# Reading 512-column operands in four passes of 16-byte granules, and moving those operands in SBUF

## The chip, the cores and the metric

The kernel runs on one core of one Trainium2 chip. The metric is device time in microseconds (us) of one execution, from the first to the last instruction with what lies around it. The time before is the median of three executions, 838.82 us (838.07 to 838.83). About 0.2% (1.7 us) is what a measurement of this kernel can tell from no change.

## The reference

One encoder layer on an input x of 512 positions by 1024 channels, all in float32:

```
x = x + 0.5 * swiglu(rms_norm(x, g1), w_gate1, w_up1, w_down1)      # 1024 -> 2752 -> 1024
u = rms_norm(x, g2) @ w_in                                          # fourier 512 | q 8x64 | k 2x64 | v 2x64
a = fourier_mixer(u[:512])                                          # Re(DFT2) per group, then a 128x128 map
b = gqa_attention(u[512:])                                          # head norms, rotary, softmax over 512 keys
x = x + concat([a, b]) @ w_out
x = x + 0.5 * swiglu(rms_norm(x, g3), w_gate2, w_up2, w_down2)
y = rms_norm(x, g4)
```

where swiglu(h, g, u, d) is (silu(h @ g) * (h @ u)) @ d.

## The kernel before

Everything is held transposed: a tile has 128 channels as its partitions and the 512 positions along them. A float32 factor is split into a high part in the matmul's own rounded format and a low part that holds the rest, and a product of two factors is three matmuls: high by high, high by low, low by high. `product` (L172) issues the three (L173, L175, L176). The stationary operand is a 128x128 block of weights, the moving one 512 positions (2048 bytes of each partition) or 256, and the result is a PSUM bank.

The layer runs in three stages.

1. The first feed-forward part (`ffn`). A first group of hidden blocks goes by plain products: `gate` multiplies the 8 pairs `hh[k]`, `hl[k]` (high and low parts of the scaled input) by weights; `opening1` does the same for the first four blocks in an order of its own (L693). All further hidden blocks go by `seven`: a seven-product scheme on half-size blocks, whose matmuls are in `multiply` (L407), with moving operands of 256 columns from the tile `rt` and weights in 4096-byte slots of the tile `ring`. Each group ends with the down products (`down`, L173 to L176, and L487 and L488 for the last 64 hidden channels), whose moving operands are the 512-column activations in the tile `at`.
2. The mixer. Six projections (`k`, `q0` to `q3`, `v`) multiply `hh` and `hl` by weights through `product`; the Fourier projections (L998 to L1000) use `hh` and `hl` as stationary operands against 256-column weights; then attention (L1134, L1135, L1160, L1203), the position transform (L1057) and the output projection.
3. The second feed-forward part, whose last group ends by halves: the last three output blocks do the first 256 positions by `product` and the rest by `by_tokens` (L519).

The order on TensorE is the order of the program text in the feed-forward parts and a list written out by hand in the mixer; it does not depend on where tiles lie.

The tile `ring` holds twelve slots for weights. `hh[k]` and `hl[k]` lie in slot k of the same tile (eight of the twelve), so weights and moving operands share it. `room(pool, n)` puts an unused tile of n bytes between others to set where the next one starts. `FURTHER` moves the Fourier weights and `SKIP` the weights of the last three down blocks, in elements of 4 bytes. In `multiply`, one matmul in each run of `seven` is cut in two, of 64 and 192 columns (`CUT`).

As built, the ring's slots start at byte 16512 of the partition, `at` at 119168 and `rt` at 148032. Taken modulo 64 all three are 0; modulo 128 `rt` lies 64 away from the slots.

Of the kernel before, what the change touches and what calls it, by code (L numbers as in the profile page):

```python
# [7 lines left out]
F32R = mybir.dt.float32r  # L8
# [5 lines left out]
P = 128  # L14
S = 512
D = 1024
KD = D // P
# [4 lines left out]
HD = 64  # L22
EPS = 1e-6
WARM = 9
FURTHER = 48
FURTHER_IN = "f0", "f1", "f2", "f3"
ROOM = 64
NS = 12

GROUPS1 = ((0, "t", 1, 2), range(3, 9), range(9, 15), range(15, 21))  # L30
# [3 lines left out]
USES = "a11", "a12", "s1", "s2", "s4", "s3", "a22"  # L34
PIECES = (0, 2, 2, 0, 2, 1, 1)
KH = KD // 2
SKIP = 16
LAST = 3
CUT = 1, P // 2
HI_DVE = ("f0", "f1")  # L40
# [43 lines left out]
def encoder(ctx, tc, A, out):  # L84
    nc = tc.nc
    cp = ctx.enter_context(tc.tile_pool(name="const", bufs=1))
    wp = ctx.enter_context(tc.tile_pool(name="weights", bufs=3))

    ring = cp.tile([P, NS * KD * P + 2 * ROOM], F32R, name="ring")
    taken = []  # L90

    def room(pool, n):


        pool.tile([P, n // 4], F32, name=f"room{len(rooms)}")
        rooms.append(n)
# [11 lines left out]
    gains = gx[:, : 4 * KD].rearrange("p (n k) -> p n k", k=KD)  # L108
    xt = gx[:, 4 * KD :].rearrange("p (k s) -> p k s", s=S)
    x = [xt[:, k, :] for k in range(KD)]  # L110
    hh = [ring[:, k * KD * P : k * KD * P + S] for k in range(KD)]
    hl = [ring[:, k * KD * P + S : (k + 1) * KD * P] for k in range(KD)]


    def in_order():
# [9 lines left out]
    def slot_at(tile, i, rooms=0):  # L125
        o = i * KD * P + rooms * ROOM
        return tile[:, o : o + KD * P]

    slots = [slot_at(ring, i, int(i >= KD + 2)) for i in range(NS)]

    def further(tile, i, rooms=0):
        o = i * KD * P + rooms * ROOM + FURTHER
        return tuple(tile[:, o + j * KD * P : o + (j + 1) * KD * P].rearrange("p (a b) -> p a b", b=P) for j in range(2))
# [21 lines left out]
    def parts_of(n):  # L155

        return (slice(0, CUT[1]), slice(CUT[1], HALF)) if n == CUT[0] else (slice(0, HALF),)

    def weights(src, name, n=KD, raw=None, by_dma=False, skip=0):
        raw = raw or raw_tile(src, name, n)  # L160
        hi, lo = weight_slots(n, skip)
        if name in HI_DVE:
            nc.vector.tensor_copy(hi[:, :n, :], raw[:, :n, :])
        else:
            nc.scalar.copy(hi[:, :n, :], raw[:, :n, :])  # L165
        if by_dma:
            rest_by_dma(lo, hi, src)
        else:
            lows(lo[:, :n, :], raw[:, :n, :], hi[:, :n, :])
        return hi, lo  # L170

    def product(ps, whi, wlo, mhi, mlo, first, last, cut=False):  # L172
        nc.tensor.matmul(ps, whi, mhi, start=first, stop=False)  # L173
        for t in parts_of(CUT[0]) if cut else (slice(0, ps.shape[-1]),):
            nc.tensor.matmul(ps[:, t], whi, mlo[:, t], start=False, stop=False)  # L175
        nc.tensor.matmul(ps, wlo, mhi, start=False, stop=last)  # L176
# [92 lines left out]
    def ffn(norm, after, wgu, wd, wdt, groups, opening, closing):  # L269
# [4 lines left out]
        n_ = norm.n  # L274
        n_plain = len(groups[0])
        with tc.tile_pool(name=f"act{n_}", bufs=1) as ap, tc.tile_pool(name=f"sums{n_}", bufs=2) as sp:
            room(ap, 192)
            at = ap.tile([P, PLACES, 2, S], F32R, name=f"at{n_}")
            room(ap, 192)
            rt = ap.tile([P, 7, 2, KH, HALF], F32R, name=f"rt{n_}")  # L280
            wt, raws = [], {}
            free, where = list(range(PLACES)), {}
# [12 lines left out]
            def gate(c, between={}, by_dma=False):  # L295
                whi, wlo = weights(wgu[c], f"gu{n_}_{c}", by_dma=by_dma)
                ps = bank(f"gu{n_}_{c}")
                for k in range(KD):
                    between.get(k, int)()
                    product(ps, whi[:, k, :], wlo[:, k, :], hh[k], hl[k], k == 0, k == KD - 1)  # L300
                return ps

            def tail_weights():
# [168 lines left out]
            def down(d, group, gi):  # L472

                js = [j for j in group if j != "t"]
                src, halves_ = wd[d][:, js[0] : js[-1] + 1, :], closing and gi == len(groups) - 1 and d >= KD - LAST
                raw = raws[d] = raw_tile(src, f"dn{n_}_{d}_{gi}", len(js))
                whi, wlo = weights(src, "", len(js), raw, skip=SKIP if halves_ else 0)
                if halves_:
                    token_weights(d, js)
                w = wt[d // 4][:, d % 4 * P : (d % 4 + 1) * P]  # L480

                def steps(ps, t):
                    for i, j in enumerate(group):
                        h, l = (at[:, where[j], o, t] for o in range(2))
                        first, last = i == 0, i == len(group) - 1
                        if j == "t":
                            nc.tensor.matmul(ps[:, t], w, h, start=first, stop=False)  # L487
                            nc.tensor.matmul(ps[:, t], w, l, start=False, stop=last)  # L488
                        else:
                            k = j - js[0]  # L490
                            cut = first and d == KD - LAST and t == slice(0, HALF)
                            product(ps[:, t], whi[:, k, :], wlo[:, k, :], h, l, first, last, cut)
                        yield

                return steps
# [36 lines left out]
            every = slice(0, S)  # L532
            for gi, group in enumerate(groups):
                last = gi == len(groups) - 1
# [3 lines left out]
                else:  # L538
# [3 lines left out]
                    pss = dict(enumerate(opening(gate, lambda: norm.column([norm.acc]), lambda: row.append(norm.row()))))  # L542
# [4 lines left out]
                    for i, c in enumerate(left):  # L547
# [6 lines left out]
                        while len(parts) * len(left) > (len(left) - 1 - i) * KH:  # L554
                            o = parts.pop(0)
# [14 lines left out]
                for d in range(KD):  # L570
# [8 lines left out]
                    ps = bank(f"dn{n_}_{d}_{gi}")  # L579
# [66 lines left out]
    cut = [0] + [4 * KD + k * S for k in (1, 2, 4, 6, 8)]  # L646
# [23 lines left out]
    def opening1(gate, column, row):  # L670

        pss = [bank(f"gu0_{c}") for c in range(4)]
        ws = []

        def highs(i, k):
            n0.scale_high(k, None if k else nc.vector)
            hi, _ = ws[i]
            for c in (slice(0, 2), slice(2, 4)) if k == 0 else (slice(0, 4),):
                nc.scalar.copy(hi[:, k % 2, c], raws[i][:, k % 2, c])

        def weight_lows(i, k):
            hi, lo = ws[i]
            lows(lo[:, k % 2], raws[i][:, k % 2], hi[:, k % 2])

        def products(k):
            hi, lo = ws[k // 2]
            passes = [(c, w, m) for w, m in ((hi, hh), (hi, hl), (lo, hh)) for c in range(4)]
            for n, (c, w, m) in enumerate(passes):
                if (k, n) == (6, 8):
                    sums()  # L690
                if (k, n) == (7, 4):
                    row()
                nc.tensor.matmul(  # L693
                    pss[c], w[:, k % 2, c], m[k], start=k == 0 and m is hh and w is hi,
                    stop=k == KD - 1 and w is lo,
                )

        ss = []

        def sums():  # L700
            ss.append(bank("ss0"))
            for c in range(4):
                n0.sum(ss[0], c, [n0.acc])

        with tc.manual_schedule(engines={mybir.EngineType.Activation, mybir.EngineType.DVE}):
            for k in range(KD):
                i = k // 2
                if k % 2 == 0:
                    ws.append(tuple(slot().rearrange("p (a c b) -> p a c b", a=2, b=P) for _ in range(2)))
                highs(i, k)  # L710
                if k < KD - 1:
                    n0.scale_low(k)
                    weight_lows(i, k)
                for j in {3: range(0, 4), 5: (4, 5), 6: (6, 7)}.get(k, ()):
                    n0.sums(j)
            for k in range(KD - 1):
                products(k)
            n0.scale_low(KD - 1)
            n0.mean(ss[0], 0, 4)
            n0.power(0, 4)  # L720
            weight_lows(KH - 1, KD - 1)
            products(KD - 1)
        nc.sync.dma_start(out=qkg, in_=A["qkg"])
        nc.sync.dma_start(out=fb, in_=A["fb"])
        return [pss[0:2], pss[2:4]]
# [6 lines left out]
    with tc.tile_pool(name="mix", bufs=1) as mp, tc.tile_pool(name="mixt", bufs=1) as mt:  # L732

        room(mp, 192)
        more_tile = mp.tile([P, 2 * KD * P + ROOM], F32R, name="more")
        more = [slot_at(more_tile, i) for i in range(2)]
# [63 lines left out]
        banks, rots, swaps, owns, sqs = {}, {}, {}, {}, {}  # L800

        def project_ops(c, name):

            weight_ops(f"w{name}", A["wins"][c])

            def step(k):
                if k == 0:
                    banks[name] = bank_for(name, {"v": 1, "k": 3, "q0": 3}.get(name, 2))
                whi, wlo = ws[f"w{name}"]
                product(banks[name], whi[:, k, :], wlo[:, k, :], hh[k], hl[k], k == 0, k == KD - 1)  # L810

            for k in range(KD):
                op(f"{name}.{k}")(lambda k=k: step(k))
# [514 lines left out]
    first, rest = out[0].rearrange("p (k s) -> p k s", s=HALF), out[1].rearrange("p (c n) -> p c n", n=D)  # L1328
# [222 lines left out]
```

## Time and profile before

| | |
|---|---|
| median of 3 executions | 838.82 us |
| span of the profiled execution | 836.5 us |
| outside the span (median less span) | 2.3 us |
| TensorE matmuls | 829.6 us busy, 99% of the span |
| VectorE | 640.0 us, 77% |
| ScalarE | 465.3 us, 56% |
| TensorE clock granted | 0.999 |

The only time of the profiled execution itself is its span; the last instructions end with it, so the 2.3 us beside it is launch and end. A matmul's own duration in the profile contains its latency: a 512-column matmul shows 389 ns, while the next one starts some 227 ns later. What a stream of matmuls costs is read from the starts in the timeline (the distance from one start to the next, here called the pace), not from the mean durations. A line of the timeline gives the start in us from the span's start, the stretch in us, the engine, the line, the operation, the tiles and the count.

### The profile page before, as it was taken

What the parts mean: (1) busy time and instruction counts of PE and PEld (TensorE: products, weight loads), DVE (VectorE), ACT (ScalarE), POOL (GpSimd) and SP (SyncE); (2) the same over time, 40 slices, a digit from 0 to 9 for tenths busy, and PEclk for the clock granted to TensorE, in tenths of its full rate; (3) what the DMA queues carried; (4) which work ended last, traced back from release to release, by engine and by line L of the source; (5) the groups of instructions that cost most, each with busy time, mean ns of one, the idle gap of its engine ahead of it and who ended that gap; (6) DMA issues with size and microseconds to landing.
All of it is one profiled execution on the core that took longest, in us unless ns stands there. A gap on an engine that the chain in (4) does not pass through costs nothing.

```text
span 836.5 us, 13664 instructions
## 1 busy us (share of the span) xinstructions
PE 829.6 (99%) x5406; PEld 751.5 (90%) x5406; DVE 640.0 (77%) x1005; ACT 465.3 (56%) x778; POOL 30.7 (4%) x34
## 2 busy tenths in 40 slices
PE   9999999999999999999999999999999999999997
PEld 6888998899989998888998888899988999899986
DVE  7898896489746947699998488999954896479573
ACT  7763664167524645677786356656622673257462
POOL 0110000000000000221100000100000000000001
PEclk9999999999999999999999999999999999999999
DMA  7664322323242213532020224443232332322222
GB/s 254 171 149 161 129 89 76 120 101 139 76 138 95 67 54 114 169 99 80 26 76 26 74 86 130 114 164 121 89 120 89 133 112 66 131 102 95 68 75 101
DMA packets 31168, 89.58 MB, mean 107 GB/s; under 512 B 3712, under 2 KB 8832, under 8 KB 31104
## 3 DMA queue, kind: packets, MB, share of 16 engines
q1 hardware_dynamic: 27776, 82.61, 29.0%
q0 software_dynamic: 2608, 5.12, 3.3%
q10 hardware_dynamic: 720, 0.98, 0.3%
q8 instruction: 42, 0.69, 0.3%
q14 instruction: 22, 0.18, 0.1%
HBM read 84.24 MB, written 2.10 MB: 103 GB/s over the span
## 4 chain that ended last, share of the span: by engine, by line
PE 98%; issue 0%; DMA 0%; DVE 0%; ACT 0%; POOLq 0%; POOL 0%; DVEq 0%
PE r L407 23%; PE q L407 11%; PE dn L175 9%; PE dn L173 9%; PE dn L176 9%; PE p L407 6%; PE mix L173 3%; PE mix L175 3%; PE mix L176 3%; PE gu L693 3%; PE gu L173 3%; PE gu L176 3%; PE gu L175 3%; PE mix L1203 2%; PE mix L1160 2%; PE mix L1134 1%
## 5 line engine op out<-in xcount | busy, mean ns | idle before, releaser
L407 PE MATMUL r<-rt,ring 128*128 128x256 f32 x1686 | 209.6, 276 | 0.0
L407 PEld LDWEIGHTS r<-rt,ring 128*128 128x128 f32 x1686 | 200.6, 188 | 0.9
L175 PE MATMUL dn<-at,ring 128*128 128x512 f32 x300 | 116.7, 389 | 0.0
L176 PE MATMUL dn<-at,ring 128*128 128x512 f32 x300 | 116.7, 389 | 0.0
L173 PE MATMUL dn<-at,ring 128*128 128x512 f32 x300 | 116.7, 389 | 0.0
L407 PE MATMUL q<-rt,ring 128*128 128x256 f32 x840 | 106.6, 276 | 0.0
L123 DVE TENSOR_TENSOR ring<-s,ring 128x1024 fp32r<-128x1024 f32 x70 | 85.5, 1221 | 24.1 <-ACT ring L366 20.8
L407 PEld LDWEIGHTS q<-rt,ring 128*128 128x128 f32 x840 | 100.4, 188 | 0.0
L528 DVE SCALAR_TENSOR_TENSOR gx<-dn,gx 128x512 f32<-128x512 f32 x61 | 41.9, 689 | 74.3 <-PE dn L176 74.3
L366 ACT CAST ring<-s 128x1024 fp32r<-128x1024 f32 x70 | 73.5, 1050 | 28.0 <-PE p L407 13.7
L165 ACT CAST ring<-raw_dn 128x768 fp32r<-128x768 f32 (+3 forms) x58 | 45.4, 786 | 76.7 <-PE dn L175 60.4
L176 PEld LDWEIGHTS dn<-at,ring 128*128 128x128 f32 x300 | 56.3, 188 | 11.8
L173 PEld LDWEIGHTS dn<-at,ring 128*128 128x128 f32 x300 | 56.3, 188 | 11.3
L175 PEld LDWEIGHTS dn<-at,ring 128*128 128x128 f32 x300 | 56.3, 188 | 11.2
L123 DVE TENSOR_TENSOR ring<-raw_dn,ring 128x768 fp32r<-128x768 f32 (+3 forms) x58 | 51.6, 892 | 5.9 <-PE r L407 4.6
L407 PE MATMUL p<-rt,ring 128*128 128x256 f32 x420 | 53.3, 276 | 0.0
L123 DVE TENSOR_TENSOR ring<-raw_g,ring 128x1024 fp32r<-128x1024 f32 x35 | 42.7, 1219 | 10.4 <-PE p L407 10.3
L407 PEld LDWEIGHTS p<-rt,ring 128*128 128x128 f32 x420 | 50.2, 188 | 0.0
L366 ACT CAST ring<-raw_g 128x1024 fp32r<-128x1024 f32 x35 | 36.8, 1053 | 13.9 <-DMA raw_g<-in_wgu 8.3
L415 ACT COPY p<-r 128x256 f32<-128x256 f32 x35 | 12.9, 370 | 49.1 <-PE r L407 48.7
L439 ACT ACTIVATE g<-g 128x512 f32<-128x512 f32 x35 | 22.2, 633 | 23.4 <-DVE g L438 23.1
L375 ACT CAST ring<-raw_u 128x512 fp32r<-128x512 f32 x35 | 21.8, 624 | 16.8 <-PE q L407 15.9
(318 smaller groups left out, 1557.1 us busy)
## 6 DMA issues: line engine op xcount, KB each, us to landing
raw_g<-in_wgu SPq DMA_DIRECT2D x35, 512.0 KB, 3.6
raw_u<-in_wgu SPq DMA_DIRECT2D x35, 512.0 KB, 4.3
raw_dn<-in_wd SPq DMA_DIRECT2D x40, 384.0 KB, 3.1
raw_gu<-in_wgu SPq DMA_DIRECT2D x12, 512.0 KB, 3.5
raw_o<-in_wo SPq DMA_DIRECT2D x8, 512.0 KB, 3.5
raw_dn<-in_wd SPq DMA_DIRECT2D x8, 448.0 KB, 3.3
raw_wq<-in_wins SPq DMA_DIRECT2D x4, 512.0 KB, 4.4
raw_f<-in_winf SPq DMA_DIRECT2D x4, 512.0 KB, 4.0
```

Of the source, the lines that this page charges most:

```text
L123: nc.vector.tensor_tensor(out=lo, in0=src, in1=asf(hi), op=ALU.subtract)
L165: nc.scalar.copy(hi[:, :n, :], raw[:, :n, :])
L173: nc.tensor.matmul(ps, whi, mhi, start=first, stop=False)
L175: nc.tensor.matmul(ps[:, t], whi, mlo[:, t], start=False, stop=False)
L176: nc.tensor.matmul(ps, wlo, mhi, start=False, stop=last)
L366: nc.scalar.copy(hi, src)
L375: nc.scalar.copy(hi, src)
L407: nc.tensor.matmul(ps[:, t], a[:, ks], b[:, i, t], start=first and i == 0 and o == 0, stop=i == KH - 1 and o == 2, skip_group_check=not first,
L439: nc.scalar.activation(b["g"], b["g"], AF.Silu)
L528: nc.vector.scalar_tensor_tensor(out=x[d][:, t], in0=ps[:, t], scalar=0.5, in1=x[d][:, t], op0=ALU.mult, op1=ALU.add)
L693: nc.tensor.matmul(pss[c], w[:, k % 2, c], m[k], start=k == 0 and m is hh and w is hi, stop=k == KD - 1 and w is lo,)
L1160: nc.tensor.transpose(pts[n][:, c * P : (c + 1) * P], prob[t, b, c][:, kc * P : (kc + 1) * P], ident)
```

## The change

The products that read a 512-column moving operand from `at`, `hh` or `hl` through `gate`, `opening1`, `down` (not its last halves) and the mixer's six projections read it, and write PSUM, in another order: instead of columns 0 to 511, four passes, each of which takes 4 columns (16 bytes) out of every 16 (64 bytes): columns 0 to 3, 16 to 19, and so on, then 4 to 7, 20 to 23, and so on. The number of columns, matmuls and weight loads stays. `hh` and `hl` start 48 bytes below the slots, and the rooms, `FURTHER` and `SKIP` are set with the same distance in mind.

```diff
-FURTHER = 48
+FURTHER = 36
+FRONT, NEAR = 16, 4
-SKIP = 16
+SKIP = 4
...
-    ring = cp.tile([P, NS * KD * P + 2 * ROOM], F32R, name="ring")
+    whole = cp.tile([P, FRONT + NS * KD * P + 2 * ROOM], F32R, name="ring")
+    ring = whole[:, FRONT:]
...
-    hh = [ring[:, k * KD * P : k * KD * P + S] for k in range(KD)]
-    hl = [ring[:, k * KD * P + S : (k + 1) * KD * P] for k in range(KD)]
+    hh, hl = (
+        [whole[:, k * KD * P + o * S + NEAR : k * KD * P + (o + 1) * S + NEAR] for k in range(KD)] for o in range(2)
+    )
...
+    def turned(ap):
+        return ap.rearrange("p (a b c) -> p b a c", b=4, c=4)
+
-    def product(ps, whi, wlo, mhi, mlo, first, last, cut=False):
+    def product(ps, whi, wlo, mhi, mlo, first, last, cut=False, turn=False):
+        if turn:
+            ps, mhi, mlo = turned(ps), turned(mhi), turned(mlo)
+            for a, b in ((whi, mhi), (whi, mlo), (wlo, mhi)):
+                nc.tensor.matmul(ps, a, b, start=first and b is mhi and a is whi, stop=last and a is wlo)
+            return
...
-            room(ap, 192)
+            room(ap, 144)
             at = ap.tile([P, PLACES, 2, S], F32R, name=f"at{n_}")
-            room(ap, 192)
+            room(ap, 240)
             rt = ap.tile([P, 7, 2, KH, HALF], F32R, name=f"rt{n_}")
...
-                    product(ps, whi[:, k, :], wlo[:, k, :], hh[k], hl[k], k == 0, k == KD - 1)
+                    product(ps, whi[:, k, :], wlo[:, k, :], hh[k], hl[k], k == 0, k == KD - 1, turn=True)
...
+                        turn = t == every
...
-                            product(ps[:, t], whi[:, k, :], wlo[:, k, :], h, l, first, last, cut)
+                            product(ps[:, t], whi[:, k, :], wlo[:, k, :], h, l, first, last, cut, turn)
...
                 nc.tensor.matmul(
-                    pss[c], w[:, k % 2, c], m[k], start=k == 0 and m is hh and w is hi,
+                    turned(pss[c]), w[:, k % 2, c], turned(m[k]), start=k == 0 and m is hh and w is hi,
...
-                product(banks[name], whi[:, k, :], wlo[:, k, :], hh[k], hl[k], k == 0, k == KD - 1)
+                product(banks[name], whi[:, k, :], wlo[:, k, :], hh[k], hl[k], k == 0, k == KD - 1, turn=True)
```

As built, the pools round every tile's size up to a multiple of 32 bytes, so the rooms of 144 and 240 bytes take 160 and 256. The places that follow, with the distance from the ring's slots modulo 64 and modulo 128:

| | slots start | `hh`, `hl` from the slots | `at` from the slots | `rt` from the slots |
|---|---|---|---|---|
| before | 16512 | 0 / 0 | 0 / 0 | 0 / 64 |
| after | 16576 | 16 / 80 | 32 / 32 | 32 / 96 |

`at` starts at 119200 after and `rt` at 148128. The order of instructions on every engine is the same in both kernels.

More of the change, by code (lines that the diff above doesn't have):

```diff
@@ L485, in steps @@
                         first, last = i == 0, i == len(group) - 1
+                        turn = t == every
                         if j == "t":
-                            nc.tensor.matmul(ps[:, t], w, h, start=first, stop=False)
-                            nc.tensor.matmul(ps[:, t], w, l, start=False, stop=last)
+                            o, h, l = (turned(p) if turn else p for p in (ps[:, t], h, l))
+                            nc.tensor.matmul(o, w, h, start=first, stop=False)
+                            nc.tensor.matmul(o, w, l, start=False, stop=last)
                         else:
```

## The prediction

> **What bounds the kernel now.** I read the page's summary and its chain first, then the groups, then the starts of single matmuls in the timeline, then windows.
>
> ```profile
> span 836.5 us, 13664 instructions
> PE 829.6 (99%) x5406; PEld 751.5 (90%) x5406; DVE 640.0 (77%) x1005; ACT 465.3 (56%) x778; POOL 30.7 (4%) x34
> ...
> PE 98%; issue 0%; DMA 0%; DVE 0%; ACT 0%; POOLq 0%; POOL 0%; DVEq 0%
> ...
> L407 PE MATMUL r<-rt,ring 128*128 128x256 f32 x1686 | 209.6, 276 | 0.0
> L407 PE MATMUL q<-rt,ring 128*128 128x256 f32 x840 | 106.6, 276 | 0.0
> L407 PE MATMUL p<-rt,ring 128*128 128x256 f32 x420 | 53.3, 276 | 0.0
> L175 PE MATMUL dn<-at,ring 128*128 128x512 f32 x300 | 116.7, 389 | 0.0
> ```
>
> TensorE's matmuls fill 99% of the span and 98% of the chain that ended last, and no matmul group of size has idle time before it. So the time is the sum of the paces of 5406 matmuls, and a change to the pace of many of them goes to the end one for one, unless another engine comes up behind. The paces are in the timeline and the chain (start, stretch, what):
>
> ```profile
> 249.79 0.39 PE L175 MATMUL dn<-at,ring 128*128 128x512 f32 x1
> 250.01 0.39 PE L176 MATMUL dn<-at,ring 128*128 128x512 f32 x1
> 250.24 0.39 PE L173 MATMUL dn<-at,ring 128*128 128x512 f32 x1
> 250.47 0.39 PE L175 MATMUL dn<-at,ring 128*128 128x512 f32 x1
> ```
>
> ```profile
> 82.85 2.72 PE r L407 x24
> ```
>
> Three 512-column matmuls take 0.68 us, 226.7 ns each; 24 of 256 columns take 2.72 us, 113.3 ns each. The second is half the first: there is no fixed cost per matmul in these streams, each column takes 0.443 ns, and one weight load per matmul hides in both. What limits them grows with the columns, which is the one thing that another order of the columns could touch.
>
> **The change, part one: the products that are reordered.** Their counts, from one row of each kind:
>
> ```profile
> L173 PE MATMUL dn<-at 128*128 128x512 f32 x15 | 5.8, 389 | 0.0
> L487 PE MATMUL dn<-at,wt 128*128 128x512 f32 x16 | 6.2, 389 | 0.0
> L173 PE MATMUL gu<-ring 128*128 128x512 f32 x72 | 28.2, 392 | 0.0
> L173 PE MATMUL gu<-ring,at 128*128 128x512 f32 x24 | 9.3, 389 | 0.0
> L693 PE MATMUL gu<-ring 128*128 128x512 f32 x48 | 11.4, 396 | 0.2 <-ACT ring L679 0.2
> L173 PE MATMUL mix<-ring 128*128 128x512 f32 x32 | 12.8, 399 | 0.0
> L173 PE MATMUL mix<-ring,more 128*128 128x512 f32 x16 | 6.5, 408 | 0.0
> ```
>
> Down: 3 x (300 + 15) and 2 x 16 for L487 and L488, 977. Gates: 3 x (72 + 24), and 2 x 48 at L693 (weights in the ring and in `at`), 384. Projections: 3 x (32 + 16), 144. Together 1505 matmuls, at 226.7 ns 341 us, 41% of the span. Nothing is added or removed; only their pace can change, and the trace holds no matmul that reads in steps. So it is bounded from both sides.
>
> Below: the transposes of attention read `ident` in order, too, at 128 columns a matmul.
>
> ```profile
> 396.72 0.60 PE L1160 MATMUL mix<-ident,e 128*128 128x128 f32 x4
> 397.30 0.50 PE L1134 MATMUL mix<-ks,qb 128*128 128x512 f32 x1
> ```
>
> ```profile
> L1160 PE MATMUL mix<-ident,e 128*128 128x128 f32 x128 | 17.7, 272 | 0.0
> ```
>
> The first four of them run from 396.72 with the last one's 0.272 us ending the stretch of 0.60, so three paces are 0.33 us and one is 109 ns: 0.85 ns a column, nearly two steps of the products' 0.443. If it is two, one step is 0.426 ns and the products lose 0.017 ns on each column; freed of that, 512 columns take 218.0 ns, 8.7 less. That is my estimate of the most that the order can bring: 1505 x 8.7 = 13.1 us.
>
> Above: 512-column matmuls that are out of step with their neighbours, here after a pause in the mixer.
>
> ```profile
> 345.65 0.40 PE L176 MATMUL mix<-ring 128*128 128x512 f32 x1
> 345.89 0.40 PE L173 MATMUL mix<-ring 128*128 128x512 f32 x1
> 346.12 0.39 PE L175 MATMUL mix<-ring 128*128 128x512 f32 x1
> 346.35 0.39 PE L176 MATMUL mix<-ring 128*128 128x512 f32 x1
> 346.58 0.40 PE L173 MATMUL mix<-ring 128*128 128x512 f32 x1
> ```
>
> Four paces take 0.93 us, 232.5 ns, 5.8 more than the settled 226.7; if every reordered product stayed there, 1505 x 5.8 = 8.7 us more. I take a saving of half the lower bound, 4.4 ns, so 6.5 us. The reasons: a loss that grows with the columns and not with the weight loads looks like one of walking through the bytes in order, which a pass over one granule in four does not do; but while the next weights are read (128 columns, as many as one pass has) two readers meet, and for the 977 down products they meet 32 bytes apart, not the 16 bytes of `hh`. Half is a choice between the bounds, nearer the gain.
>
> Cover: with the products shorter, the gate stage has little beside it.
>
> ```profile
> 25.00:55.00 30.00, 30.00 (x135) 24.62 (x134) 28.14 (x50) 22.80 (x31) 6.63 (x6) 1.00 0.74 165
> ```
>
> In that window of gates (its length, then TensorE, its weight loads, VectorE, ScalarE, GpSimd, the clock) VectorE is busy 28.14 of 30 us, so TensorE can gain 1.9 us of 30 there, 6%; 4.4 of 226.7 is 2%, so it fits. The clock (1.00) has nothing to give. The waits and the queues are as before: the order of instructions on every engine is the same, and the shifted `hh`, which now reach 48 bytes into the slot below, are written where that slot's weights have been used.
>
> **Part two: the products that are not reordered.** `rt` was meant to stay; as built it lies 32 bytes off the slots modulo 64, where it lay at 0. L407 has 1686 + 840 + 420 = 2946 matmuls, 40% of the span at 113.3 ns. That distance matters: the same line has a slower pace when it is out of step, and the one line whose moving operand lies 32 bytes off its weights (the 256-column sines of `pos` at L1057: `pos` starts at 135808, a multiple of 64, and they at its element 1032, 1288 or 1544, each 32 bytes past one) shows that pace, too.
>
> ```profile
> 135.74 1.58 PE L407 MATMUL r<-rt,ring 128*128 128x256 f32 x12
> 137.15 0.39 PE L173 MATMUL dn<-at,ring 128*128 128x512 f32 x1
> ```
>
> ```profile
> 441.65 0.40 PE L1057 MATMUL mix<-pos,eh 128*128 128x256 f32 x2
> 441.89 0.28 PE L1057 MATMUL mix<-pos,el 128*128 128x256 f32 x1
> 442.01 0.28 PE L1057 MATMUL mix<-pos,eh 128*128 128x256 f32 x1
> 442.12 0.39 PE L1134 MATMUL mix<-ks,qb 128*128 128x512 f32 x1
> ```
>
> Twelve matmuls of L407 take 137.15 - 135.74 = 1.41 us, 117.5 ns each; four of L1057 take 0.47 us, 117.5 ns each. Both are 4.2 ns over 113.3. I take the row that it is nearest to: all of L407 at 117.5, 2946 x 4.2 = 12.4 us more. The bounds are nothing (the four sines come right after other unsettled matmuls, so they do not prove that the distance holds them there) and twice that, 24.8, if both readers collide again within one matmul.
>
> Small: the 63 matmuls of 256 columns in the last halves keep neither their distance of 64 bytes nor a whole line (16 bytes less 32), 63 x 4.2 = 0.3 us; L519's 42, whose stationary operand `at` moves and whose moving one does not, may fall either way by 4.2 ns, 0.2 us, counted as nothing. The Fourier products and the channel products move both operands alike: nothing.
>
> ```profile
> L519 PE MATMUL last<-ring,at 128*128 128x384 f32 x42 | 8.5, 346 | 0.0
> L173 PE MATMUL last<-at,ring 128*128 128x256 f32 x21 | 5.8, 277 | 0.0
> ```
>
> **The sum.** -6.5 + 12.4 + 0.3 = 6.2 us on the profile's 836.5, so a span of 842.7. The 2.3 us between span and median (838.8) is untouched: **845.0 us**.
>
> [...]
>
> **The rivals.**
>
> *It is faster: L407 keeps its pace.* The mechanism is that the distance of 32 bytes costs nothing in a long settled stream, and only the pause before the sines made them slow. For it: L407 itself falls out of step at the same addresses (the twelve above) and back. Against: the sines have the slower pace of L407 to the tenth of a nanosecond. Then the sum is -6.5 + 0.3, 832.6 us; with the whole 8.7 ns, 826.0. It decides at a loss of 6.2 / 2946 = 2.1 ns per L407 matmul: under that the change gains. It also wins if L407 pays 4.2 and the reordered products save more than 12.7 / 1505 = 8.4 ns, just inside the bound. Together 0.32.
>
> *Steps cost.* Each jump between granules, in SBUF or PSUM, costs something instead of saving. If each of the four passes pays one loss of 4.2 ns, a product takes 243.5 ns: 1505 x 16.8 = 25.3 us, with L407's 12.4 and 0.3 it is 876.8. For it: each matmul that met a reader out of step paid just this. Against: a granule is read whole, so the count of 16-byte pieces is the same. At one column's step (0.443 ns) per jump and 128 jumps it would be 85.3 us instead of 25.3, 936.8. Chance 0.20.
>
> *Nothing moves.* The loss per column is in the array or its inputs and not in the order, and L407 finds its pace again: 838.8 to 840. Chance 0.08, of which 0.07 is within 0.2%.
>
> **How the numbers follow.** The forecast's case (some gain on 1505, L407 at about 117.5) has 0.40 and spans, by its bounds of 8.7 ns saved and 5.8 lost, 838.4 to 860.2, nearly all of it above 840.5. Faster by over 0.2% has 0.32, from the first rival; slower has 0.38 of the forecast's 0.40 (its lower end reaches into no change), 0.20 and the last 0.01 of the third, 0.59; same has 0.02 + 0.07, 0.09. The range reaches down to 826, the end of the first rival, and up to 877, the price of the second; left out is L407's double loss and dearer jumps. The likeliest case alone is 838 to 860.
>
> **What would show it.** In the changed profile the chain stays TensorE's at 98%. The starts of L407 should lie 117.5 ns apart (2.82 us for 24, not 2.72); those of the down products 222 ns apart. L407 at 113.3 makes the first rival; down products over 232.5 make the second. Should VectorE end waits in the gate window, the cover was too thin. I am wrong in the mechanism, whatever the time, if both paces stay at 226.7 and 113.3.

## The result and the profile after

The changed kernel takes 851.84 us (851.25 to 852.10, four executions) against 838.52 us for the kernel before in the same session: a ratio of 1.0159, 95% interval 1.0145 to 1.0172, 13.3 us more. The forecast was 845.0 us with 826 to 877 around it: the direction is right and the time lies inside the range, but the forecast change, 6.2 us, is less than half of the measured one. The granted clock of the two profiled executions is the same (0.999 before, 1.000 after).

The page of the changed kernel, the first parts that answer to those of before, then two groups:

```profile
span 850.1 us, 13668 instructions
PE 843.2 (99%) x5406; PEld 765.3 (90%) x5406; DVE 642.1 (76%) x1005; ACT 466.9 (55%) x778; POOL 30.8 (4%) x34
...
PE 98%; issue 0%; DMA 0%; DVE 0%; ACT 0%; POOLq 0%; POOL 0%; DVEq 0%
PE dn L182 25%; PE r L418 23%; PE q L418 12%; PE gu L182 8%; PE p L418 6%; PE mix L182 4%; PE gu L706 3%; PE mix L187 2%; PE mix L186 2%; PE mix L184 2%; PE mix L1216 2%; PE mix L1173 2%; PE mix L1147 1%; PE mix L1013 1%; PE mix L1148 1%; PE mix L1011 1%
...
L418 PE MATMUL r<-rt,ring 128*128 128x256 f32 x1686 | 217.5, 281 | 0.0
L182 PE MATMUL dn<-at,ring 128*128 128x512 f32 x900 | 209.0, 387 | 0.0
```

TensorE is still 98% of the chain and waits for no other engine; L418 is what L407 was, and the stepped products all stand at L182 (and L706 for `opening1`, L500 and L501 for the last 64 channels). The same 1686 matmuls of `r` fill 217.5 us instead of 209.6, without idle time. So the loss is pace, and the timeline gives it. Each line has start, stretch, and count; the distance to the next line's start divided by the count is the pace.

```profile
28.71 11.37 PE L182 MATMUL gu<-ring 128*128 128x512 f32 x48
39.92 5.67 PE L182 MATMUL gu<-ring,at 128*128 128x512 f32 x24
45.44 10.73 PE L182 MATMUL gu<-ring 128*128 128x512 f32 x48
56.01 0.87 PE L182 MATMUL dn<-at 128*128 128x512 f32 x3
...
139.83 28.74 PE L182 MATMUL dn<-at,ring 128*128 128x512 f32 x126
168.41 1.68 PE L418 MATMUL r<-rt,ring 128*128 128x256 f32 x13
169.93 1.58 PE L418 MATMUL p<-rt,ring 128*128 128x256 f32 x12
171.35 1.58 PE L418 MATMUL q<-rt,ring 128*128 128x256 f32 x12
172.77 1.58 PE L418 MATMUL r<-rt,ring 128*128 128x256 f32 x12
...
343.26 8.10 PE L182 MATMUL mix<-ring 128*128 128x512 f32 x36
351.19 0.95 PE L240 MATMUL mix<-ones,acc 128*128 128x2 f32 x8
```

The stepped products have three paces. Gates with weights in the ring: 10.57 us / 48 = 220.2 ns; projections: 7.93 / 36 = 220.3 ns. Down products: 28.58 / 126 = 226.8 ns, what they took in order. Gates with weights in `at`: 5.52 / 24 = 230.0 ns. One run of 48 gates with weights in the ring, the first line, does not fit: 11.21 / 48 = 233.5 ns. And L418 runs at 1.42 / 12 = 118.3 ns instead of 113.3.

What differs among the three is the distance between the two operands. From here on it is counted from the moving operand up to the weights that are loaded beside it, modulo 64. (The table under "The change" counts the other way, so its 16 is 48 here. Its 32 for `at` after the change, modulo 128, should be 96: 119200 - 16576 = 801 x 128 + 96. Nothing below rests on that entry.) With the starts of all matmuls in the trace grouped by it, the changed kernel's sum over the kernel before, pauses left out, is:

| matmuls | distance | count | mean pace, before | after | difference, us |
|---|---|---|---|---|---|
| stepped, gates and projections | 48 | 400 | 227.2 | 222.0 | -2.1 |
| stepped, gates with weights in `at` | 16 | 119 | 227.2 | 230.4 | +0.4 |
| stepped, down | 32 | 932 | 227.2 | 226.9 | -0.3 |
| L407, in order | 32 | 2934 | 113.6 | 118.4 | +14.1 |
| last halves, 256 columns | 48 | 63 | 113.6 | 117.8 | +0.3 |

Products without a row here, such as the few down products that take both operands from `at` (distance 0, 226.9 ns after and 226.7 before), add next to nothing. Together the rows are 12.4 of the 13.6 us between the two spans. The changed places, not the changed order, made the loss, if this reading holds. The experiments test it.

### The profile page after: what moved, and what is told of

Its sections match the earlier page's. It is cut to its first block, busy times and chain, and to the rows that moved or that the text cites. A ratio compares the mean times of both kernels' runs of the same rounds, so it can differ in the third digit from the quotient of the medians.

```text
span 850.1 us, 13668 instructions
## 1 busy us (share of the span) xinstructions
PE 843.2 (99%) x5406; PEld 765.3 (90%) x5406; DVE 642.1 (76%) x1005; ACT 466.9 (55%) x778; POOL 30.8 (4%) x34
## 4 chain that ended last, share of the span: by engine, by line
PE 98%; issue 0%; DMA 0%; DVE 0%; ACT 0%; POOLq 0%; POOL 0%; DVEq 0%
PE dn L182 25%; PE r L418 23%; PE q L418 12%; PE gu L182 8%; PE p L418 6%; PE mix L182 4%; PE gu L706 3%; PE mix L187 2%; PE mix L186 2%; PE mix L184 2%; PE mix L1216 2%; PE mix L1173 2%; PE mix L1147 1%; PE mix L1013 1%; PE mix L1148 1%; PE mix L1011 1%
## 5 line engine op out<-in xcount | busy, mean ns | idle before, releaser
L418 PE MATMUL r<-rt,ring 128*128 128x256 f32 x1686 | 217.5, 281 | 0.0
L182 PE MATMUL dn<-at,ring 128*128 128x512 f32 x900 | 209.0, 387 | 0.0
L418 PEld LDWEIGHTS r<-rt,ring 128*128 128x128 f32 x1686 | 208.0, 188 | 1.0
L182 PEld LDWEIGHTS dn<-at,ring 128*128 128x128 f32 x900 | 167.6, 187 | 35.5 <-DVE ring L126 0.9
L418 PE MATMUL q<-rt,ring 128*128 128x256 f32 x840 | 110.8, 281 | 0.0
L418 PEld LDWEIGHTS q<-rt,ring 128*128 128x128 f32 x840 | 104.3, 188 | 0.0
L418 PE MATMUL p<-rt,ring 128*128 128x256 f32 x420 | 55.4, 281 | 0.0
L418 PEld LDWEIGHTS p<-rt,ring 128*128 128x128 f32 x420 | 52.2, 188 | 0.0
L182 PE MATMUL gu<-ring 128*128 128x512 f32 x216 | 49.6, 384 | 0.0
L182 PEld LDWEIGHTS gu<-ring 128*128 128x128 f32 x216 | 40.4, 188 | 7.6
L463 DVE TENSOR_TENSOR u<-g,u 128x512 f32<-128x512 f32 x35 | 24.0, 686 | 6.6 <-ACT u L462 6.6
L254 POOL TENSOR_TENSOR r<-ms,mhalf 128x4 f32<-128x4 f32 (+1 forms) x4 | 4.3, 1072 | 682.8 <-DVE ms L247 682.8
```

Source lines behind the costliest of these rows:

```text
L182: nc.tensor.matmul(ps, a, b, start=first and b is mhi and a is whi, stop=last and a is wlo)
L418: nc.tensor.matmul(ps[:, t], a[:, ks], b[:, i, t], start=first and i == 0 and o == 0, stop=i == KH - 1 and o == 2, skip_group_check=not first,
L463: nc.vector.tensor_tensor(out=u, in0=b["g"], in1=u, op=ALU.mult)
```

## The experiments

Theory P: the loss is the place of `rt`, which the rounding of tile sizes moved by 32 bytes, and the missing gain is the place of `at`. The rival, theory C: the stepped products leave the matmul stream out of step and L407 inherits it.

**The places as they were meant** (e1_meant):

```diff
-            room(ap, 144)
-            at = ap.tile([P, PLACES, 2, S], F32R, name=f"at{n_}")
-            room(ap, 240)
+            room(ap, 128)
+            at = ap.tile([P, FRONT + PLACES * 2 * S], F32R, name=f"at{n_}")
+            at = at[:, NEAR : NEAR + PLACES * 2 * S].rearrange("p (m o s) -> p m o s", o=2, s=S)
+            room(ap, 192)
```

> The changed kernel with `at` really 48 bytes below the slots' grid (the tile is 64 bytes longer and sliced at element 4) and `rt` back 64 bytes off it modulo 128. Theory P (place): L407's slower pace comes from `rt` lying 32 bytes off, and the stepped down products lose their saving by lying 32 instead of 48 bytes off; then L407 returns to 113.5 ns, 1331 stepped products (down, most gates, projections) take 220 to 222 ns, and the time is 838.5 - 1505 x 5 to 6.5 = 829 to 831 us. Theory C (carry): the stepped products leave the stream out of phase and L407 inherits it whatever its place; then L407 stays near 118 ns and the time near 845 us.

830.41 us, ratio 0.9899 (0.9884 to 0.9914): faster than the kernel before by 8.4 us. Its timeline at the same place:

```profile
136.35 27.88 PE L182 MATMUL dn<-at,ring 128*128 128x512 f32 x126
164.07 1.65 PE L419 MATMUL r<-rt,ring 128*128 128x256 f32 x13
165.56 1.52 PE L419 MATMUL p<-rt,ring 128*128 128x256 f32 x12
166.92 1.52 PE L419 MATMUL q<-rt,ring 128*128 128x256 f32 x12
```

Down: 27.72 / 126 = 220.0 ns. L419 (L407 before): 1.36 / 12 = 113.3 ns. Both went back with their places, as theory P has it. The stepped 1331 at distance 48 have a mean of 220.2; 163 are at distance 0, with 229.7.

**The rooms alone** (e2_rooms_alone): the kernel before with 144 and 240 bytes.

```diff
-            room(ap, 192)
+            room(ap, 144)
...
-            room(ap, 192)
+            room(ap, 240)
```

> The kernel before with the rooms of 144 and 240 bytes alone: all products in column order, `at` and `rt` 32 bytes off the slots. Theory P: L407 at 118.4 ns, so 2946 x 5 = 14.7 us for it, and the down products, in order at 32 bytes, near 231 ns, 4 us more: 853 to 858 us. Theory C: no stepped product, so L407 at 113.5 and the time 838 to 840 us.

859.78 us, ratio 1.0248 (1.0233 to 1.0264). Two views of it, the timeline and the chain:

```profile
249.62 0.40 PE L175 MATMUL dn<-at,ring 128*128 128x512 f32 x1
249.85 0.40 PE L176 MATMUL dn<-at,ring 128*128 128x512 f32 x1
250.08 0.40 PE L173 MATMUL dn<-at,ring 128*128 128x512 f32 x1
250.32 0.40 PE L175 MATMUL dn<-at,ring 128*128 128x512 f32 x1
```

```profile
757.47 2.84 PE r L407 x24
```

24 matmuls of L407 take 2.84 us, 118.3 ns, with no stepped product in the kernel, so the steps are not needed to slow it. The run does not tell the place of `rt` from what runs ahead of it, though: here that is down products in order at 233 ns, and e13_place_alone below has L407 slow behind such products in its old place, too. e3_rt_back tells the two apart. The down products, in order at 32 bytes, take 0.70 / 3 = 233 ns, six more than at 0. The changed kernel's 227 there is therefore a saving of 6 ns by the order against a loss of 6 by the place.

**`rt` back, `at` left at 32** (e3_rt_back):

```diff
-            room(ap, 240)
+            room(ap, 224)
```

> The changed kernel with the second room at 224 bytes, so that `rt` lies 64 bytes off modulo 128 as before and `at` stays 32 bytes off. Theory P: L407 at 113.5, the down products as in the changed kernel (227 ns): 851.8 - 14.5 = 837 us. Theory C: 849 to 852 us.

838.44 us, ratio 0.9991 (0.9976 to 1.0005).

```profile
136.47 28.70 PE L182 MATMUL dn<-at,ring 128*128 128x512 f32 x126
165.01 1.66 PE L418 MATMUL r<-rt,ring 128*128 128x256 f32 x13
166.51 1.52 PE L418 MATMUL p<-rt,ring 128*128 128x256 f32 x12
167.87 1.52 PE L418 MATMUL q<-rt,ring 128*128 128x256 f32 x12
```

L418 is back at 1.36 / 12 = 113.3 ns behind down products that still take 28.54 / 126 = 226.5 ns. In the changed kernel the products ahead had the same pace (226.8), so the place of `rt` alone makes the difference. One edit of 16 bytes in a filler tile, 32 as built, is worth 13.4 us, all of the loss.

The time is 1.4 us over the expected 837, and its executions spread from 836.4 to 841.0. L418 is issued in six long runs of 407 to 491 matmuls and in groups of 12 between down products. In the profiled execution (838.81 us) five of the long runs stand at 113.4 ns, and one, at the same distance and behind the same kind of products, stands at 117.8 from its start to its end:

```profile
550.43 1.68 PE L418 MATMUL r<-rt,ring 128*128 128x256 f32 x13
551.95 1.58 PE L418 MATMUL p<-rt,ring 128*128 128x256 f32 x12
```

So L418 has two settled paces in its old place. One long run at the slower costs 491 x 4.4 ns = 2.2 us, which is about the step between the executions (836.4 to 837.0, 838.4 to 838.8, 841.0); only one of them was profiled, so that is a reading.

**The order alone** (e4_order_alone): every tile where it was, products stepped (`FURTHER`, `SKIP` and the rooms as before, `NEAR` 16).

> The stepped order alone, every tile where it lay before (distance 0 for the stepped products). Theory P: stepped products at 225 ns as the few at distance 0 in the changed kernel, L407 at 113.5: 838.5 - 1505 x 1.7 = 836 us. Theory C: L407 at 118 again, 850 us.

836.51 us, ratio 0.9963 (0.9949 to 0.9978).

```profile
136.35 28.32 PE L182 MATMUL dn<-at,ring 128*128 128x512 f32 x126
164.51 1.65 PE L418 MATMUL r<-rt,ring 128*128 128x256 f32 x13
```

28.16 / 126 = 223.5 ns here, 224.4 over all stepped products: the order saves at distance 0, too, though less than half as much as at 48. One of the five executions took 851.55 us and left no trace; the ratio leaves it out.

**Which side pays: SBUF or PSUM** (e5_read_only, e6_write_only). The first steps the moving operand alone, in the places of e1_meant; the second steps PSUM alone, in the places of before. Each leaves out the other half of the order, so the columns of its result come out permuted, and it serves for the time alone. The edit below is the one in `product`; the two other places that issue stepped products have the same.

```diff
-            ps, mhi, mlo = turned(ps), turned(mhi), turned(mlo)
+            mhi, mlo = turned(mhi), turned(mlo)      # e5_read_only
+            ps = turned(ps)                          # e6_write_only
```

> e1_meant with the stepped order on the moving operand alone; PSUM is written in order, so the columns of those products come out permuted. Theory R (the saving is in reading SBUF): stepped products stay at 220 ns and the time near 830.4 us. Theory W (the order of the PSUM writes matters, for better or worse): they go to another pace; at 226.7 ns, the pace in order, it is 838 us.

> e4_order_alone with the stepped order on PSUM alone; the moving operand is read in order at distance 0, so again the columns come out permuted. Theory R: the products keep the 226.7 ns of the kernel before, 838.5 to 839.5 us. [...]

830.68 us (ratio 0.9906, 0.9885 to 0.9928) and 838.56 us (1.0000, 0.9989 to 1.0011). In windows of down products (length, TensorE busy with its count, clock, share of the DMA engines, GB/s), e5_read_only has

```profile
140.00:160.00 20.00, 20.00 (x93) 1.00 0.45 145
```

and e6_write_only

```profile
140.00:160.00 20.00, 20.00 (x90) 1.00 0.45 148
```

93 matmuls touch the 20 us, as in e1_meant, against 90 in order. The saving is in how SBUF is read: it stays without the steps in PSUM and is gone with those steps alone. The steps in PSUM, granules of four, cost nothing that the times show: with them alone ten down products take 2.27 us (163.66 to 165.93 in its timeline), 227 ns each, against 226.7 in the kernel before.

**The other 2946** (e7_seven_too, e9_seven_0, e10_seven_32, e11_seven_two): L407 stepped as well, at three distances, and once in two passes. The edit is that of e7_seven_too against e1_meant; e9_seven_0 and e10_seven_32 have 0 and 8 for `NEAR` in it.

```diff
-            rt = ap.tile([P, 7, 2, KH, HALF], F32R, name=f"rt{n_}")
+            rt = ap.tile([P, FRONT + 14 * KH * HALF], F32R, name=f"rt{n_}")
+            rt = rt[:, NEAR : NEAR + 14 * KH * HALF].rearrange("p (n o k s) -> p n o k s", o=2, k=KH, s=HALF)
...
-                                    ps[:, t], a[:, ks], b[:, i, t], start=first and i == 0 and o == 0,
+                                    turned(ps[:, t]), a[:, ks], turned(b[:, i, t]), start=first and i == 0 and o == 0,
```

> e1_meant with L407's 256-column matmuls in the same four passes (64 columns a pass) and `rt` 16 bytes above a multiple of 64, so that its distance is 48, too. Theory H (the saving needs three of four passes free of a weight load; a load is as long as 128 columns, two passes here): half the share or less, 111.5 to 113.3 ns a matmul, 825 to 830 us. Theory F (the saving is per column): 110.1 ns, 2946 x 3.3 = 9.7 us less, 820.5 us. If the steps of 64 columns lose: over 113.3 ns, above 831 us.

> e7_seven_too with `rt` 16 bytes lower, so that L407's stepped matmuls lie 64 bytes (0 modulo 64) from the slots. If distance 48 was the wrong one for passes of 64 columns, the pace falls under 113 ns here: below 830 us. If a stepped matmul of 256 columns has no room beside its weight load, no distance helps: 114 ns or more, 832 us or more.

> The same at a distance of 32 bytes. Under 113 ns (below 830 us) if it is a matter of distance alone; 114 ns or more if not.

> e7_seven_too with two passes of 16-byte granules out of every 32 bytes for L407, so that a pass has 128 columns again but visits two of the four 16-byte places of 64 bytes. If the length of a pass counts: 110 to 112 ns, below 827 us. If keeping to one 16-byte place counts, as e8_two_passes says for wider granules: 115 ns or more, above 835 us.

834.61 (ratio 0.9946, 0.9930 to 0.9962), 836.19 (0.9953, 0.9936 to 0.9970), 834.48 (0.9948, 0.9927 to 0.9968) and 844.89 us (1.0072, 1.0051 to 1.0093), all slower than e1_meant. In e7_seven_too:

```profile
166.03 1.53 PE L420 MATMUL p<-rt,ring 128*128 128x256 f32 x12
167.40 1.54 PE L420 MATMUL q<-rt,ring 128*128 128x256 f32 x12
168.78 1.53 PE L420 MATMUL r<-rt,ring 128*128 128x256 f32 x12
```

114.6 ns (2.75 / 24), over the 113.3 in order, and the means are 114.4 and 114.7 at the other distances: a matmul of 256 columns gains from the order at none of them. In two passes of 16 out of 32 bytes it is 117.4. Theory H of e7_seven_too was too kind by a little: no share is saved, 1 ns is lost. The single paces repeat in fives, 109, 117, 117, 115, 115: one matmul in five is faster than the 113.3 in order, and the other four are slower.

**Two passes of 32 bytes** (e8_two_passes):

```diff
-        return ap.rearrange("p (a b c) -> p b a c", b=4, c=4)
+        return ap.rearrange("p (a b c) -> p b a c", b=2, c=8)
```

> e1_meant with two passes of 32-byte granules (8 columns out of every 16) instead of four of 16 bytes. If what counts is that a pass keeps to one 16-byte column of the 64-byte grid, the saving shrinks by half or is lost: 223 to 231 ns, 834 to 845 us. If any order that steps 64 bytes does it: 220 ns, 830 us.

855.95 us, ratio 1.0201 (1.0185 to 1.0217), worse than all that I had written.

```profile
141.00 29.36 PE L182 MATMUL dn<-at,ring 128*128 128x512 f32 x126
170.20 1.68 PE L419 MATMUL r<-rt,ring 128*128 128x256 f32 x13
171.71 1.58 PE L419 MATMUL p<-rt,ring 128*128 128x256 f32 x12
173.13 1.58 PE L419 MATMUL q<-rt,ring 128*128 128x256 f32 x12
```

Down: 29.20 / 126 = 231.7 ns. And L419 is at 1.42 / 12 = 118.3 ns although `rt` lies where it lies in e1_meant. Here theory C seems to have its case, products out of step that hand it on. But only five of the six long runs of L419 stand at that pace (mean 117.8); the other one does not, behind the same two-pass products:

```profile
564.92 1.52 PE L419 MATMUL p<-rt,ring 128*128 128x256 f32 x12
566.28 1.52 PE L419 MATMUL q<-rt,ring 128*128 128x256 f32 x12
```

1.36 / 12 = 113.3 ns. So the products ahead do not settle it by themselves.

**The places alone** (e13_place_alone): e1_meant with every product in order.

```diff
-        return ap.rearrange("p (a b c) -> p b a c", b=4, c=4)
+        return ap
```

> e1_meant with every product in column order, so that only the places differ from the kernel before (`at`, `hh`, `hl` 48 bytes below the slots' grid, `rt` unmoved). If the distance of 48 bytes is what saves, the 512-column products take 220 ns and the time is 830 us. If the order saves and the distance only lets it: in order they collide with the weight load as at 32 bytes, 233 ns, 1494 x 6 = 9 us over the kernel before, 847 us.

859.08 us, ratio 1.0245 (1.0213 to 1.0277).

```profile
170.35 1.69 PE L419 MATMUL r<-rt,ring 128*128 128x256 f32 x13
171.88 1.58 PE L419 MATMUL p<-rt,ring 128*128 128x256 f32 x12
173.29 1.58 PE L419 MATMUL q<-rt,ring 128*128 128x256 f32 x12
174.70 1.58 PE L419 MATMUL r<-rt,ring 128*128 128x256 f32 x12
```

In order at distance 48 the 512-column products take 233.6 ns (mean of 1331): the distance without the order is a loss of 6, the order with it a gain of 7. I had expected 847, which counted the products alone: they are some 9 of the 19.4 us that the profiled execution (857.95 us) has over the kernel before. Another 10 (2934 x 3.4) are L419, in its old place: its mean is 117.0. In the lines above it has 1.41 / 12 = 117.5 ns, and five of its six long runs stand at 117.8, but again not the sixth:

```profile
565.92 1.52 PE L419 MATMUL p<-rt,ring 128*128 128x256 f32 x12
567.28 1.52 PE L419 MATMUL q<-rt,ring 128*128 128x256 f32 x12
```

That is 113.3 ns, and its groups of 12 between down products of 234.7 ns have about 114.

**A version with more of it** (e12_best): the gate weights in `at` moved up by 48 bytes, so that they lie at distance 48, and the output projection stepped, with its weights moved up by 48 bytes.

```diff
+            at_whole = at
...
-                    lent = [at[:, i].rearrange("p a b -> p (a b)") for i in range(PLACES - 4, PLACES)]
+                    lent = [at_whole[:, FRONT + i * 2 * S : FRONT + (i + 1) * 2 * S] for i in range(PLACES - 4, PLACES)]
...
-                product(banks[name], whi[:, k, :], wlo[:, k, :], *m, k == 0, k == KD - 1)
+                product(banks[name], whi[:, k, :], wlo[:, k, :], *m, k == 0, k == KD - 1, turn=True)
```

> e1_meant with two more groups at distance 48: the gate weights that lie in `at` (moved up by 48 bytes) and the output projection (192 matmuls, stepped, its weights moved up by 48 bytes). By the paces of e1_meant: 163 x (229.7 - 220.2) + 192 x (228.6 - 220.2) = 3.2 us less than 830.4: 827 us. If output weights moved or stepped gain nothing: 829 us.

829.61 us, ratio 0.9894 (0.9872 to 0.9916).

```profile
38.91 5.44 PE L182 MATMUL gu<-ring,at 128*128 128x512 f32 x24
44.19 2.14 PE L182 MATMUL gu<-ring 128*128 128x512 f32 x9
```

The gates with weights in `at` went to 5.28 / 24 = 220.0 ns, and all 1683 stepped products have a mean of 220.2. For the output projection only the weights were moved; its moving operands lie on multiples of 64, those of e1_meant 16 bytes above one, and a distance of 48 gives 220 ns with both. The profiled execution, at 828.57 us, is 2.5 under that of e1_meant, but the medians differ by 0.8 and the intervals overlap: the paces are as expected, the gain over e1_meant is not shown by the times.

The paces together, with pauses left out (means over all matmuls of the kind; a mean can mix settled paces, as e13_place_alone's 233.6 does, with 230.0 ns in most gates and the first down products and 234.7 in the later down products):

| columns, order | distance | mean pace, ns | kernel |
|---|---|---|---|
| 512 in order | 0 | 227.2 | before |
| | 32 | 233.2 | e2_rooms_alone |
| | 48 | 233.6 | e13_place_alone |
| 512, four passes of 16 bytes | 0 | 224.4 | e4_order_alone |
| | 16 | 230.4 | changed kernel |
| | 32 | 226.9 | changed kernel |
| | 48 | 220.2 | e1_meant |
| 512, two passes of 32 bytes | 48 | 231.7 | e8_two_passes |
| 256 in order | 0 (64 modulo 128) | 113.6 | before |
| | 32 | 118.4 | changed kernel |
| 256, four passes of 16 bytes | 0 / 32 / 48 | 114.4 / 114.7 / 114.7 | e9, e10, e7 |

## Why the prediction was right or wrong, point by point

**What bounds the kernel.** Right. TensorE carried 97% or 98% of the chain in both kernels and in e12_best, and the paces account for 12.4 of the 13.6 us between the spans.

**Part two, L407 out of place: right in mechanism, small in size.** The forecast saw that `rt` had been moved by the rounding, and priced it by the four sines at 117.5 ns, 4.2 over. It measured 118.4 against 113.6 as means, 4.8 more: 14.1 us instead of 12.4. e3_rt_back shows that term by itself, 13.4 us. That the price came so near has some luck in it. The sines' 0.47 us is read to a hundredth, so four of them give a pace to 2 or 3 ns and not "to the tenth", and L407 has 117.8 ns out of step in its old place, too, so such a pace does not by itself tell of a distance.

**Part one, the stepped products: this term of the sum was mis-sized.** The step that failed is "I take a saving of half the lower bound, 4.4 ns", for all 1505, whatever their distance. It measured -2.1, +0.4 and -0.3 us in the three groups, 2.0 us in all instead of 6.5. The step named the distance of the down products as a reason for halving, and then gave them the same half as the others; e1_meant and e2_rooms_alone show that they had 6.8 ns to win at 48 bytes and that 32 bytes took all of it. The step also took all of `hh` as lying at one distance, though the gates with weights in `at` have another one (16, where they lost 3 ns). The two misses, 4.5 and 1.7 us, are 6.2 of the 7.1 us between forecast and result.

**The bounds.** The lower one, 218.0 ns from the transposes, held: the best settled pace is 220.0. Its working, that a transpose takes two steps a column, was tested by no run, so the nearness may be luck. The upper bound, 232.5 ns from products out of step, lies near the paces in order at a wrong distance (233.2 and 233.6) and in granules of 32 bytes (231.7).

**The reasons.** That the loss comes of walking through the bytes in order fits e5_read_only, where the saving is on the side that is read (830.68 us, against 838.56 in e6_write_only). That two readers meet while the next weights are read was the author's argument, and no run took the load away. What was measured fits it: stepped products have 220.2 ns at 48 bytes (e1_meant), 226.9 at 32 and 230.4 at 16 (the changed kernel), and L407's matmuls, which gain nothing (114.4 to 114.7 ns stepped, 113.6 in order), have more of a load beside them. In the kernel before, weight loads are busy for all 20.00 us from 170 to 190, in L407, and for 16.57 of the 20.00 us from 140 to 160, in down products. A load's own record is 188 ns in both; how much of that time it reads SBUF was not shown.

**Cover, waits and queues.** Right: in the changed kernel no matmul waited for VectorE (TensorE's one wait in its trace is 0.8 us, at L651, for its own sequencer), and e1_meant ran the gates at 220 ns with VectorE's work beside it and a single wait for it of 0.2 us.

**The rivals.** That L407 keeps its pace did not happen: 32 bytes cost it 4.8 ns in all six long runs. What that rival leaned on, that L407 can be out of step at unchanged addresses, is real all the same and fills whole runs, at 117.8 ns, in e3_rt_back, e8_two_passes and e13_place_alone. That each step costs something did not happen: at equal distance the 512-column products in four passes were never slower than in order (224.4 ns against 227.2 at 0, 226.9 against 233.2 at 32, 220.2 against 233.6 at 48; 16 was not run in order), and the 256-column matmuls lost 1 ns (114.4 to 114.7 against 113.6). Nor did steps in PSUM, in granules of four, cost anything: e6_write_only has a ratio of 1.0000 and 227 ns a down product. The other way to a gain, a saving of 8.4 ns a product with L407 slow, was out of reach: the best group gained 7.0.

## What to carry to other kernels

Where TensorE's stream is the whole time, look at the pace by the addresses of both operands before and after an edit, as built and not as written: a filler tile that was rounded from 240 to 256 bytes cost 13 us here, and with the other one, rounded from 144 to 160, it turned a gain of 1% into a loss of 1.6%. An access order and a place are one choice: 512-column operands of 4-byte elements read in four passes of 16 bytes gained 3% of their pace at one of the four distances that were run, and the same place without the order lost 3%. Price such a term separately for each distance that the built kernel has.

## What the runs showed of the hardware that was not expected

A settled stream of 512-column matmuls can run at 220.0 ns (0.430 ns a column) instead of 226.7 (0.443), by the order and the place in which SBUF is read; the order alone brings it to 223.5. A matmul of 256 columns gained nothing at any of three distances (114.4 to 114.7 ns, against 113.6 in order).

L407 has two settled paces in its old place, 113.4 and 117.8 ns, and a long run of it (407 to 491 matmuls) keeps one from its start to its end. All six long runs had the faster one behind products in order at 226.7 ns and behind stepped ones at 220.0 and 223.5, five of six behind stepped ones at 226.5 (e3_rt_back), and one of six behind in-order ones at 230.0 to 234.7 (e13_place_alone) and behind two-pass ones at 231.7 (e8_two_passes). With `rt` 32 bytes off, all six stand at 118.4, in the changed kernel and in e2_rooms_alone. So the place sets what paces there are, and what runs ahead seems to bear on which of them a run takes. What decides it is open, and so is why 48 is the best of the four distances.

The distance modulo 64 does not tell all, either: stepped products at 0 have 224.4 ns in e4_order_alone, where both operands lie on multiples of 64, but the 163 of e1_meant, where both lie 16 bytes above one, have 229.7.
